# Scatter steps in one row and one branch for a pair's second block, in an expert stage on one core

## The chip, the cores and the metric

One of the eight cores of a Trainium2 chip runs the whole program. The metric is the device time of one execution in microseconds (us); a time without a name is a median over the runs.

## The reference, cut to what matters

Two layers of a diffusion backbone on 512 tokens of width 1024, in fp32. Layer 0 mixes tokens by a gated DeltaNet, layer 1 by a short gated convolution; after each mixer comes a mixture of SwiGLU experts, and a last RMSNorm ends the whole. The change lies in the experts alone. A router gives each token 2 of 32 experts, so 1024 rows of work in all. Expert e does, for its rows h (normed and modulated), with w1 and w3 of 1024 x 512 and w2 of 512 x 1024:

```
y = (silu(h @ w1[e]) * (h @ w3[e])) @ w2[e]
x[token] += weight * gate * y
```

## The kernel before, in words

`moe(l)` (L1454) runs once a layer: layer 0 from about 620 to 1130 us, layer 1 from about 1361 to 1865. The code is written out pair by pair for 16 pairs of experts. Pair p holds experts 2p and 2p + 1. Of each expert 64 rows stand in the pair's **first block** (128 rows); the two experts use two halves of 64 columns of TensorE at the same time, so each product is a row of matmuls that alternate between x = 0 and 1. If an expert of the pair has more than 64 rows (`n > 64`), a **second block** of 128 rows is computed too, under `tc.If`, a branch that every engine takes for itself. In this data that is so for 2 of the 30 pairs of the loop: pair 12 of layer 0 and pair 4 of layer 1. Pair 15 stands behind the loop and isn't changed.

A first block goes through these steps, with the lines at which the trace shows the work:
- **gate_up** (L1493, ends in ACT's Silu, L1499): 32 matmuls of h with w1 of both experts.
- **lin_up** (L1493, ends in DVE's product g = lin * silu, L1502): 32 matmuls with w3. `side` lets other steps run between them: the matmuls come in eight groups (k = 0 to 7), and a step stands behind each k that is named.
- **turn_g** (L1508, L1510): four transposes of g and a copy by ACT.
- **turn** (L1479, L1485 on DVE and its like on ACT): the next pair's gathered rows hg, transposed by eight matmuls and modulated into hT.
- **down** (L1520): 32 matmuls with w2; then DVE weighs the result, ACT and POOL split it into yhi and ylo (L1530, L1531).
- **scatter** of the pair's result, done within the next pair: eight steps, each of two matmuls with a selection matrix (L1556 yhi, L1557 ylo) into a PSUM bank and an add by DVE into the tokens xs (L1558).

All weights come in **units** of one 128 x 4096 tile: per pair two of w1, two of w3, two of w2, one for each expert. Nine buffers in three rings hold them. `issue(done)` (L162) goes through a fixed order of units and sends on SP's queue the load of every next unit (`load_unit`, L215) whose ring has a buffer that is free once the units before number `done` are used up. `next_unit(hold)` calls `issue(taken - hold)` and hands out the next unit. On the chip the load waits by semaphore until the engine that read the buffer is done; where the reader stands under a branch that isn't taken, PE raises the semaphore when it passes the branch.

The order of the instructions on each engine is the order of the code (a manual schedule). A pair of before:
1. next_unit twice (reissues the down buffers of pair p - 1), gate_up;
2. branch 1 (L1626): turn of hx to hTx, gate_up of the second block into gx;
3. next_unit twice (reissues the two gate buffers), lin_up with scatter steps of pair p - 1 behind groups 1, 3 and 5;
4. branch 2 (L1633): lin_up of the second block;
5. gather of hg for pair p + 2 on POOL, `issue(taken)` (reissues the two lin buffers), the five scatter steps left;
6. next_unit twice, out() (new yhi, ylo, sel);
7. branch 3 (L1642): turn_g, down and scatter of the second block;
8. turn_g, turn of the next rows, more(p + 2) (reads the count of pair p + 2 and gathers its second rows if there are any), down.

After the loop, a branch at L1665 covers the blocks beyond the second ones (`rest`), and isn't taken here.

Of the kernel before, what the change touches and what calls it, by code (L numbers as in the profile page):

```python
# [34 lines left out]
class Net:  # L35
# [83 lines left out]
    def plan(self):  # L119
# [18 lines left out]
        def moe(l):  # L138
            for p in range(16):
                for n in ("w1", "w3", "w2"):  # L140
                    order.extend((n, l, 2 * p + x) for x in range(2))
        moe(0)
        for g in range(2):
            order.extend(("w_in_b", 3072, u + g, 0) for u in (0, 2, 4))
            if g == 0:
                order.extend(("ada_w", 6144, 4 * b + u, l) for l, b in self.later for u in range(4))
        order.extend(("w_out_b", 1024, u, 0) for u in range(2))
        moe(1)

        self.place = {o: "B" for o in order if o[0] in ("ada_w", "w_in_b") or o[:2] == ("w2", 0) and o[2] > 29}  # L150
# [1303 lines left out]
    def moe(self, l):  # L1454
        tc, nc, I = self.tc, self.nc, self.I
        with ExitStack() as ms:
# [7 lines left out]
            def gather(gi, hg=None, skip=False, of=None):  # L1464

                if hg is None:
                    hg = wk.tile([128, 1024], F32, name="hg", bufs=2)
                of = self.hscr if of is None else of
                nc.gpsimd.indirect_dma_start(out=hg, out_offset=None, in_=of[:, :],
                                             in_offset=bass.IndirectOffsetOnAxis(ap=gi, axis=0),  # L1470
                                             **(dict(bounds_check=of.shape[0] - 1, oob_is_err=False) if skip else {}))
                return hg

            def turn(hg, to=None):

                hT = (wk.tile([128, 1024], F32, name="hT") if to is None else to).rearrange("p (k d) -> p k d", k=8)
                ps = [self.bank("tr") for _ in range(2)]
                for c in range(8):
                    nc.tensor.transpose(ps[c // 4][:, 128 * (c % 4):128 * (c % 4) + 128], hg[:, c::8], self.ident)  # L1479
                for c in range(8):  # L1480
                    q = ps[c // 4][:, 128 * (c % 4):128 * (c % 4) + 128]
                    if c > 3:
                        nc.scalar.activation(hT[:, c], q, AF.Identity, bias=self.m8[:, l, 2, c:c + 1], scale=self.m8[:, l, 0, c:c + 1])  # L1483
                    else:
                        nc.vector.tensor_scalar(hT[:, c], q, self.m8[:, l, 0, c:c + 1], self.m8[:, l, 2, c:c + 1], op0=OP.mult, op1=OP.add)  # L1485
                return hT

            def up(hT, w, side=()):

                ps = self.bank("pj")  # L1490
                for k in range(8):
                    for x in range(2):
                        nc.tensor.matmul(ps[64 * x:64 * x + 64], hT[:, k, 64 * x:64 * x + 64], w[x][:, k], start=(k == 0), stop=(k == 7))  # L1493
                    for _ in range(side[1].count(k) if side else 0):
                        next(side[0], None)
                return ps

            def gate_up(hT, w, g, side=()):
                nc.scalar.activation(g, up(hT, w, side), AF.Silu)  # L1499

            def lin_up(hT, w, g, side=()):
                nc.vector.tensor_tensor(g, up(hT, w, side), g, op=OP.mult)  # L1502

            def turn_g(g, gT=None):

                pg = self.bank("tr")
                for k in range(4):
                    nc.tensor.transpose(pg[:, 128 * k:128 * k + 128], g[:, k::4], self.ident)  # L1508
                gT = wk.tile([128, 4, 128], F32, name="gT") if gT is None else gT[:, :512].rearrange("p (k d) -> p k d", k=4)
                nc.scalar.activation(gT, pg.rearrange("p (k d) -> p k d", k=4), AF.Copy)  # L1510
                return gT

            def down(gT, w, ti, wi, o, y, eng=nc.gpsimd):

                self.sel(o, ti)
                for n in range(2):
                    py = self.bank("pj")
                    for k in range(4):
                        for x in range(2):
                            nc.tensor.matmul(py[64 * x:64 * x + 64], gT[:, k, 64 * x:64 * x + 64], w[x][:, k, 512 * n:512 * n + 512],  # L1520
                                             start=(k == 0), stop=(k == 3))
                    weigh(py, n, wi, y)
                    split(n, o, y, eng)
# [17 lines left out]
            def ident(x1):  # L1541
                for t in range(4):
                    nc.tensor.matmul(x1[t], self.ident, self.xs[:, t, 512:], start=True, stop=False)
                    yield

            def scatter(*a):
                for _ in scatter_parts(*a):
                    pass

            def scatter_parts(yhi, ylo, sel, ns=(0, 1)):  # L1550
                for n in ns:
                    for t in range(4):
                        ps = self.bank("pj")
                        c = slice(512 * n, 512 * n + 512)
                        s = sel[:, 128 * t:128 * t + 128]
                        nc.tensor.matmul(ps, s, yhi[:, c], start=True, stop=False)  # L1556
                        nc.tensor.matmul(ps, s, ylo[:, c], start=False, stop=True)  # L1557
                        nc.vector.tensor_tensor(self.xs[:, t, c], ps, self.xs[:, t, c], op=OP.add)  # L1558
                        yield n, t

            def col(t, c):
                return t[:, c:c + 1]

            gx = wk.tile([128, 512], F32, name="gx")

            def out():
                return tuple(wk.tile([128, m], F32R, name=n) for n, m in (("yhi", 1024), ("ylo", 1024), ("sel", 512)))

            def count(p):
                return nc.values_load(self.cnt[0:1, p], min_val=0, max_val=512)  # L1570
            hx = [wk.tile([128, 1024], F32, name=f"hx{i}") for i in range(2)]

            def more(p):
                n = count(slice(p, p + 1))
                with tc.If(n > 64):
                    gather(col(self.gxc, 16 + p), hx[p % 2])
                return n
# [33 lines left out]
            hgs = [gather(col(self.gxc, p)) for p in range(2)]  # L1611
# [3 lines left out]
            hT = turn(hgs.pop(0))  # L1615
# [4 lines left out]
            prev = None  # L1620
            for p in range(15):
                n = ns.pop(p)
                w = self.next_unit(), self.next_unit(1)
                g = wk.tile([128, 512], F32, name="g")
                gate_up(hT, w, g, () if p else (route, range(8)))
                with tc.If(n > 64):  # L1626

                    hTx = turn(hx[p % 2], hx[p % 2])
                    gate_up(hTx, w, gx)
                w = self.next_unit(), self.next_unit(1)  # L1630
                add = scatter_parts(*prev) if prev else iter(())
                lin_up(hT, w, g, (add, (1, 3, 5)))
                with tc.If(n > 64):  # L1633
                    lin_up(hTx, w, gx)
                if p < 14:
                    hgs.append(gather(col(self.gix, p + 2), skip=True))
                    self.issue(self.taken)
                for _ in add:
                    pass
                w = self.next_unit(), self.next_unit(1)  # L1640
                prev = out()
                with tc.If(n > 64):  # L1642
                    down(turn_g(gx, hx[p % 2]), w, col(self.tid, 16 + p), col(self.wsl, 16 + p), prev, gx)
                    scatter(*prev)
                gT = turn_g(g)
                hT = turn(hgs.pop(0))
                if p < 13:
                    ns[p + 2] = more(p + 2)
                prev = out()
                down(gT, w, col(self.tid, p), col(self.wsl, p), prev, g, nc.gpsimd if p < 14 else nc.vector)  # L1650

            n = count(slice(15, 16))
            w = self.next_unit(), self.next_unit(1)
            g = wk.tile([128, 512], F32, name="g")
            add = scatter_parts(*prev, ns=(1, 0))
            gate_up(hT, w, g, (add, (2, 3, 3, 4, 5, 6, 7)))
            w = self.next_unit(), self.next_unit(1)
            x1 = [self.bank("pj") for _ in range(4)]
            add = chain(add, ident(x1))
# [17 lines left out]
            prev = out()  # L1677
# [252 lines left out]
```

## Time and profile before

| what | before |
|---|---|
| median of 3 runs | 1875.29 us |
| the runs | 1871.93 to 1875.86 us |
| the profiled execution | 1876.28 us |
| its span in the trace | 1874.2 us |
| mean granted clock of TensorE in it | 0.964 of full speed |

The rest of the profile is a page and a trace of that one execution. Times in its rows count from the start of the span. The engines are PE (TensorE matmuls), PEld (its weight loads), DVE, ACT, POOL and SP; a q behind a name (PEq, SPq) is the engine's sequencer, which issues DMAs, branches and semaphore events. L1493 is line 1493 of the kernel.

### The profile page before, as it was taken

What the parts mean: (1) busy time and instruction counts of PE and PEld (TensorE: products, weight loads), DVE (VectorE), ACT (ScalarE), POOL (GpSimd) and SP (SyncE); (2) the same over time, 40 slices, a digit from 0 to 9 for tenths busy, and PEclk for the clock granted to TensorE, in tenths of its full rate; (3) what the DMA queues carried; (4) which work ended last, traced back from release to release, by engine and by line L of the source; (5) the groups of instructions that cost most, each with busy time, mean ns of one, the idle gap of its engine ahead of it and who ended that gap; (6) DMA issues with size and microseconds to landing.
All of it is one profiled execution on the core that took longest, in us unless ns stands there. A gap on an engine that the chain in (4) does not pass through costs nothing. (4 is left out here: it accounts for less than half of the span.)

```text
span 1874.2 us, 26554 instructions
## 1 busy us (share of the span) xinstructions
PE 1709.8 (91%) x10229; PEld 977.8 (52%) x10230; DVE 814.8 (43%) x1611; ACT 483.3 (26%) x888; POOL 415.4 (22%) x297
## 2 busy tenths in 40 slices
PE   5999988997988799999999988999799999999997
PEld 4766667776866344434434336688534344344332
DVE  5435877746664332323323237633523233233233
ACT  4465354523223111111111115223211111111112
POOL 1114464635410101111010103343111111110100
PEclk9999989998998899999999998999899999999998
DMA  9569975779835899999998953714589969999993
GB/s 330 192 241 339 293 222 157 173 170 262 244 107 227 345 425 425 427 425 426 426 425 346 404 193 139 279 40 180 226 340 427 425 268 425 426 425 425 426 418 123
DMA packets 154551, 572.33 MB, mean 305 GB/s; under 512 B 55208, under 2 KB 79961, under 8 KB 126214
## 3 DMA queue, kind: packets, MB, share of 16 engines
q1 hardware_dynamic: 148326, 555.26, 77.6%
q0 software_dynamic: 4896, 10.48, 1.5%
q10 hardware_dynamic: 1152, 4.19, 0.5%
q8 instruction: 115, 1.88, 0.4%
q14 instruction: 62, 0.51, 0.1%
HBM read 550.86 MB, written 26.38 MB: 308 GB/s over the span
## 5 line engine op out<-in xcount | busy, mean ns | idle before, releaser
L1493 PE MATMUL pj<-w,hT 128*64 128x512 f32 x2048 | 482.7, 602 | 7.1 <-DMA w<-in_w 2.5
L1558 DVE TENSOR_TENSOR xs<-pj,xs 128x512 f32<-128x512 f32 x264 | 170.5, 687 | 372.9 <-PE pj L1557 369.1
L1493 PEld LDWEIGHTS pj<-w,hT 128*64 128x64 f32 x2048 | 151.4, 137 | 266.1 <-issue 251.3
L1531 POOL TENSOR_TENSOR ylo<-g,yhi 128x512 fp32r<-128x512 f32 x56 | 70.8, 1265 | 653.4 <-ACT yhi L1530 653.4
L1520 PE MATMUL pj<-w,gT 128*64 128x512 f32 x960 | 212.6, 594 | 3.0 <-DVE hT L1485 1.6
L666 POOL TENSOR_TENSOR wlo<-w,whi 128x1024 fp32r<-128x1024 f32 x43 | 106.5, 2479 | 230.2 <-ACT whi L664 228.7
L1520 PEld LDWEIGHTS pj<-w,gT 128*64 128x64 f32 x960 | 78.1, 137 | 116.5 <-issue 108.8
L1526 DVE SCALAR_TENSOR_TENSOR g<-pj,wsl,gate 128x512 f32<-128x512 f32 x64 | 48.0, 751 | 177.7 <-PE pj L1520 164.1
L1556 PE MATMUL pj<-yhi,sel 128*128 128x512 f32 x264 | 117.5, 445 | 4.9 <-PEq L1633 4.2
L1510 ACT ACTIVATE gT<-tr 128x512 f32<-128x512 f32 x32 | 19.1, 598 | 383.5 <-PE tr L1508 383.5
L1556 PEld LDWEIGHTS pj<-yhi,sel 128*128 128x128 f32 x264 | 49.4, 187 | 120.0 <-issue 90.4
L681 PE MATMUL pj<-w,whi 128*128 128x512 f32 x336 | 105.7, 394 | 0.6 <-ACT whi L664 0.6
L1557 PE MATMUL pj<-ylo,sel 128*128 128x512 f32 x264 | 104.3, 395 | 1.3 <-POOL ylo L1531 1.3
L681 PE MATMUL pj<-hhi,wlo 128*128 128x512 f32 x224 | 93.7, 419 | 8.3 <-POOL wlo L666 7.0
L681 PE MATMUL pj<-hhi,whi 128*128 128x512 f32 x224 | 93.4, 417 | 6.4 <-DVE cv L797 5.5
L681 PE MATMUL pj<-hlo,whi 128*128 128x512 f32 x224 | 91.5, 409 | 0.0
L1530 ACT ACTIVATE yhi<-g 128x512 fp32r<-128x512 f32 x62 | 39.2, 632 | 193.3 <-DVE g L1526 193.3
L681 PEld LDWEIGHTS pj<-w,whi 128*128 128x128 f32 x336 | 63.7, 190 | 15.2 <-ACT whi L664 1.0
L664 ACT ACTIVATE whi<-w 128x1024 fp32r<-128x1024 f32 x53 | 55.3, 1054 | 53.9 <-PE pj L681 37.6
L1499 ACT ACTIVATE g<-pj 128x512 f32<-128x512 f32 x32 | 19.1, 598 | 190.5 <-PEq L1626 141.1
L681 PE MATMUL pj<-w,wlo 128*128 128x512 f32 x168 | 66.3, 394 | 0.0
L1483 ACT ACTIVATE hT<-tr,m 128x128 f32<-128x128 f32 x128 | 48.3, 458 | 55.2 <-PE tr L1479 53.5
(613 smaller groups left out, 2692.1 us busy)
## 6 DMA issues: line engine op xcount, KB each, us to landing
w<-in_w SPq DMA_DIRECT2D x188, 2048.0 KB
w<-in_ada_w SPq DMA_DIRECT2D x20, 2048.0 KB
w<-in_w_in_a SPq DMA_DIRECT2D x8, 2048.0 KB
w<-in_w_in_b SPq DMA_DIRECT2D x6, 2048.0 KB
w<-in_ada_w SPq DMA_DIRECT2D x8, 1024.0 KB
w<-in_w SPq DMA_DIRECT2D x8, 1024.0 KB
Y<-R SPq DMA_DIRECT2D x20, 256.0 KB
vp<-vscr SPq DMA_DIRECT2D x18, 256.0 KB
```

Of the source, the lines that this page charges most:

```text
L664: nc.scalar.activation(hi[:, :, :n], w, AF.Copy)
L666: (lo_eng or nc.gpsimd).tensor_tensor(lo[:, :, :n], w, hi[:, :, :n].bitcast(F32), op=OP.subtract)
L681: nc.tensor.matmul(out, n[j][0][:, k], n[j][1][:, k, a:b], start=(i == 0), stop=(i == 23))
L1483: nc.scalar.activation(hT[:, c], q, AF.Identity, bias=self.m8[:, l, 2, c:c + 1], scale=self.m8[:, l, 0, c:c + 1])
L1493: nc.tensor.matmul(ps[64 * x:64 * x + 64], hT[:, k, 64 * x:64 * x + 64], w[x][:, k], start=(k == 0), stop=(k == 7))
L1520: nc.tensor.matmul(py[64 * x:64 * x + 64], gT[:, k, 64 * x:64 * x + 64], w[x][:, k, 512 * n:512 * n + 512], start=(k == 0), stop=(k == 3))
L1526: nc.vector.scalar_tensor_tensor(y, py, wi, self.gate[:, 512 * n:512 * n + 512], op0=OP.mult, op1=OP.mult)
L1530: nc.scalar.activation(o[0][:, c], y, AF.Copy)
L1531: eng.tensor_tensor(o[1][:, c], y, o[0][:, c].bitcast(F32), op=OP.subtract)
L1556: nc.tensor.matmul(ps, s, yhi[:, c], start=True, stop=False)
L1557: nc.tensor.matmul(ps, s, ylo[:, c], start=False, stop=True)
L1558: nc.vector.tensor_tensor(self.xs[:, t, c], ps, self.xs[:, t, c], op=OP.add)
```

## The change

It touches the loop over pairs 0 to 14 alone. Behind gate_up, lin_up runs without side work; then come the gather for p + 2, all eight scatter steps of pair p - 1, and out(). One branch holds the whole second block: turn, gate_up, lin_up, turn_g, down and scatter. The four units of lin and down are taken with a hold of 2 to 5, so that none of these calls reissues a buffer of this pair, and `issue(self.taken - 4)` finds none either. `issue(self.taken - 2)` behind the branch reissues the four buffers of gate and lin.

```diff
                 gate_up(hT, w, g, () if p else (route, range(8)))
+                wl = self.next_unit(2), self.next_unit(3)
+                lin_up(hT, wl, g)
+                if p < 14:
+                    hgs.append(gather(col(self.gix, p + 2), skip=True))
+                    self.issue(self.taken - 4)
+                if prev:
+                    scatter(*prev)
+                wd = self.next_unit(4), self.next_unit(5)
+                prev = out()
                 with tc.If(n > 64):
 
                     hTx = turn(hx[p % 2], hx[p % 2])
                     gate_up(hTx, w, gx)
-                w = self.next_unit(), self.next_unit(1)
-                add = scatter_parts(*prev) if prev else iter(())
-                lin_up(hT, w, g, (add, (1, 3, 5)))
-                with tc.If(n > 64):
-                    lin_up(hTx, w, gx)
-                if p < 14:
-                    hgs.append(gather(col(self.gix, p + 2), skip=True))
-                    self.issue(self.taken)
-                for _ in add:
-                    pass
-                w = self.next_unit(), self.next_unit(1)
-                prev = out()
-                with tc.If(n > 64):
+                    lin_up(hTx, wl, gx)
+                    w = wd
                     down(turn_g(gx, hx[p % 2]), w, col(self.tid, 16 + p), col(self.wsl, 16 + p), prev, gx)
                     scatter(*prev)
+                w = wd
+                self.issue(self.taken - 2)
                 gT = turn_g(g)
```

## Rows read from the trace of the kernel before

**Rows 1.** The page: part 1 (engines), part 2 (40 slices), part 6 (DMA issues).

```profile
PE 1709.8 (91%) x10229; PEld 977.8 (52%) x10230; DVE 814.8 (43%) x1611; ACT 483.3 (26%) x888; POOL 415.4 (22%) x297
...
DMA  9569975779835899999998953714589969999993
...
w<-in_w SPq DMA_DIRECT2D x188, 2048.0 KB
```

**Rows 2.** Windows: from:to, us, busy PE, PEld, DVE, ACT, POOL; PEclk, DMA share, GB/s.

```profile
639.00:951.00 312.00, 300.13 (x1334) 127.02 (x1330) 95.07 (x168) 43.67 (x88) 39.82 (x34) 1.00 1.01 426
...
1373.60:1375.80 2.20, 2.10 (x10) 0.79 (x8) 0.07 (x1) 0.47 (x1) 0.00 (x0) 1.00 0.03 7
1531.00:1535.80 4.80, 4.80 (x26) 1.97 (x24) 0.75 (x1) 0.63 (x1) 1.27 (x1) 1.00 0.00 0
1535.80:1537.80 2.00, 2.00 (x12) 0.71 (x10) 0.75 (x1) 0.63 (x1) 0.36 (x1) 1.00 0.65 147
...
1539.80:1829.00 289.20, 281.60 (x1250) 115.93 (x1246) 94.49 (x165) 39.71 (x80) 30.87 (x27) 1.00 1.00 424
```

**Rows 3.** Timeline of PE, one pair: start, us, operation, count, idle before and its releaser.

```profile
652.46 9.15 PE L1493 MATMUL pj<-w,hT 128*64 128x512 f32 x40
661.54 0.50 PE L1556 MATMUL pj<-yhi,sel 128*128 128x512 f32 x1
...
662.20 1.94 PE L1493 MATMUL pj<-w,hT 128*64 128x512 f32 x8
...
669.36 0.47 PE L1556 MATMUL pj<-yhi,sel 128*128 128x512 f32 x1 [0.16 <-PEq L1633]
...
672.04 0.72 PE L1508 MATMUL tr<-ident,g 128*128 128x128 f32 x4
...
674.23 7.09 PE L1520 MATMUL pj<-w,gT 128*64 128x512 f32 x32
681.12 1.45 PE L1493 MATMUL pj<-w,hT 128*64 128x512 f32 x5
```

**Rows 4.** Timeline of PE: pair 11, taken pairs, last pairs, the branch L1665.

```profile
951.62 3.08 PE L1493 MATMUL pj<-w,hT 128*64 128x512 f32 x6 [2.46 <-DMA w<-in_w]
...
974.68 7.07 PE L1493 MATMUL pj<-w,hT 128*64 128x512 f32 x32
...
1010.26 7.09 PE L1520 MATMUL pj<-w,hx 128*64 128x512 f32 x32 [0.69 <-ACT hx L1510]
...
1118.20 2.83 PE L1538 MATMUL pj<-w,gT 128*64 128x512 f32 x6 [5.21 <-PEq L1665]
...
1479.27 7.07 PE L1493 MATMUL pj<-w,hT 128*64 128x512 f32 x32
...
1800.78 1.94 PE L1493 MATMUL pj<-w,hT 128*64 128x512 f32 x8 [0.16 <-PEq L1626]
```

**Rows 5.** Timeline of SP's queue: refills of weight buffers, two at a time.

```profile
635.12 0.82 SPq L215 DMA_DIRECT2D w<-in_w  x2
...
642.50 0.80 SPq L215 DMA_DIRECT2D w<-in_w  x2
...
659.65 0.81 SPq L215 DMA_DIRECT2D w<-in_w  x2
...
1375.82 0.81 SPq L215 DMA_DIRECT2D w<-in_w  x2
...
1383.20 0.81 SPq L215 DMA_DIRECT2D w<-in_w  x2
...
1535.82 0.81 SPq L215 DMA_DIRECT2D w<-in_w  x2
...
1542.82 0.80 SPq L215 DMA_DIRECT2D w<-in_w  x2
```

**Rows 6.** Timeline of DVE: the adds of the five scatter steps in a row.

```profile
670.16 3.08 DVE L1558 TENSOR_TENSOR xs<-pj,xs 128x512 f32<-128x512 f32 x5
```

**Rows 7.** One line, L1665: count, ns (least/median/most), first and last start.

```profile
L1665 PEldq COMPARE_BRANCH  x2: 3591/4913/6235, 1111.5 to 1845.5; - x2
```

## The prediction, made before the change was run

> **What bounds the kernel now.** I began with the page's shares and slices [rows 1]: PE works 91% of the span, and the DMA row holds two long stretches of nines, which are the expert stages of the two layers. The windows over them [rows 2] say more than the mean: from 639 to 951 us and from 1539.8 to 1829 the DMA engines are busy at a share of 1.00 or more, at 424 to 426 GB/s, without a break, while PE is busy 96 to 97% of the same time. Two limits run side by side there. A pair loads six units of 2.097 MB (2048 KB an issue [rows 1]) and a gather of about 0.5 MB: 13.1 MB, at 425 GB/s **30.8 us**. PE's pair, read from the timeline of a pair whose second block is skipped, lasts 681.12 - 652.46 = **28.66 us** [rows 3]. So PE eats up, pair after pair, the lead that the nine buffers gave it at the start of a layer. In layer 0 the lead is gone at 951.62: PE waits 2.46 us for the second lin unit of pair 11, and the six matmuls behind the wait take 3.08 us where 6 x 0.215 = 1.29 is usual [rows 4] (1.8 us more). In layer 1 the taken second block comes early (pair 4, from 1479.27), the queue drains meanwhile (0 GB/s from 1531 to 1535.8 [rows 2]) and starts afresh; no wait for weights shows, but the lead is nearly used up at the end. I check that by counting. From the first refill of layer 0, whose transfer starts some 2 us after its issue at 635.12 [rows 5], to the landing at 951.62 there are 61 units: 314.4 us, 5.15 us a unit. From 1537.8 (restart in layer 1) to the second lin unit of pair 14 there are 51 units: 262.7 us, so it lands at 1800.5; that product starts (its last part, after the branch) at 1800.78 [rows 4]. Slack there: 0.3 us by this count, and I allow 0 to 1.2.
>
> What follows from this: in layer 0 up to pair 11, and in layer 1 from pair 5 to pair 14, what the transfers do decides, and time saved on PE is worth nothing by itself. Only pairs after these points, and pairs 0 to 3 of layer 1, turn PE time into time.
>
> **The change, part by part.**
>
> PE, pair not taken (28 of 30). A product of 32 matmuls with nothing between takes 681.12 - 674.23 = 6.89 [rows 3]. Before, gate, the first branch and 8 lin matmuls take 661.54 - 652.46 = 9.08, against 40 x 0.215 = 8.61: 0.47 for the branch and the change of operands. Five steps in a row with the third branch take 672.04 - 669.36 = 2.68, at most 0.54 a step; one between the lin matmuls costs 662.20 - 661.54 = 0.66 and another change behind it. After: three products 20.67, five steps and one branch 2.68, three more steps at 0.54 1.61, and the unchanged stretch from turn_g to down 674.23 - 672.04 = 2.19: together 27.15. **Saving 1.5 us a pair.** Pair 0 of a layer has nothing to scatter and saves only the 0.47.
>
> DVE and PSUM. The adds of five steps take 3.08, 0.62 each [rows 6], PE's step 0.54 or less, so eight adds trail PE by some 1.5 us at the end of the row. The 2.19 of turn_g and turn cover that; the transposed g doesn't wait for them, the half of hT that DVE evacuates may, by 0 to 0.6. I take 0.2 and leave it inside the rounding. Without that cover the price is the 1.5.
>
> POOL: the gather for p+2 is issued one branch earlier, and costs nothing as before. SP: the instructions are the same, six issues a pair; what moves is when they can go. This is the main term.
>
> **The refills.** Before, the two buffers of gate were reissued when gate and its branch were over (659.65 in the pair of rows 3, 7.2 us into it), those of lin after the second branch. Now next_unit is called with a hold of 2 to 5, so it issues nothing, and all four go with issue(taken - 2) behind the single branch, 18 us into the pair. Where the DMA queue still holds other units, this costs nothing: five units of later work stand in it then. It costs where the queue is empty: at the first refill of a layer, and after the taken pair.
> - Layer 0: the first refill goes at about 642.2 (lin's end and the branch; its own refill went at 642.50) in place of 635.12 [rows 5]: **+7.0** on the whole unbroken chain of transfers. PE's pairs 1 to 10 save nothing, they wait more. Pair 11's lin starts at 951.62 + 7.0. The rest of that pair saves 1.15 (three interleaved steps and two branches): +5.85 at pair 12's gate. Its lin now follows gate at once, at 974.68 + 5.85 + 6.9 = 987.4, and its second unit lands 30.8 after the last one: 989.4 by the mean; 0 to 2, I take +1.0.
> - Pair 12, taken: it saves the interleaving, about 0.9. It pays where the scatter steps covered something: turn_g of gx follows lin_up of gx directly and waits for DVE's product; today five steps stand there and still 0.69 is left before the down product at 1010.26 [rows 4]. I take +1.0 (0.69 for the product, and the hand-over), and +0.7 for the turn of hx, whose DVE half now stands behind eight adds. Sum +0.8. Pairs 13 and 14: -1.5 each. Layer 0: 7.0 - 1.15 + 1.0 + 0.8 - 3.0 = **+4.65**, from 2.5 to 6.5.
> - Layer 1, start: the queue is really empty there (7 GB/s from 1373.6 to 1375.8 [rows 2]). First refill 1375.82, now 0.3 before the second of today (1383.20 [rows 5]): +7.1 on the chain. PE saves 0.5 + 3 x 1.5 = 5.0 until pair 4's gate, 1474.3; lin wants its second unit at 1481.2. Nineteen units of 5.15 from 1378 give 1475.9, with the delay 1483.0: a wait of 1.8, and up to 1.8 more as after 951.62; I take 2.5. Pair 4 itself +0.8, as above. So its end, and the refill of its down buffers (1535.82 before), comes at 1535.82 - 5.0 + 2.5 + 0.8 = 1534.1.
> - Layer 1, after the taken pair: its gate and lin refills can still go inside the block, as before, but all of them have landed when the block ends. The two down units are read by 1534.1 + 2 + 10.3 = 1546.4. Before, the next two came at 1542.82, in time. Now four come together at pair 5's branch: 1533.3 + 2 x 6.89 + 4.3 + 0.3 = 1551.7, and pick-up takes 2 (147 GB/s in the first two us of the restart before). The queue is empty for 7.3, and the chain stands at -1.7 + 7.3 = **+5.6**, from 4 to 7. Less the slack of 0.3 to 1.2: +4.9 to 5.3 at pair 14's lin, whose rest saves 1.0. Layer 1: **+4.2**, from 2 (less slack lost) to 8 (a slow stretch of 1.8 behind one or two waits).
>
> Sum: 4.65 + 4.2 = **+8.9 us**. The profiled execution took 1876.28 us, its span 1874.2 and 2.1 around it; the median of the runs is 1875.29, 1.0 lower. 1876.28 + 8.9 = 1885.2, by the median **1884.2**.
>
> **The price of the single branch.** No row shows a skip of this size: it passes over 124 matmuls with 124 weight loads, against 52 and 52 for the longest of today, inside the 2.68. The near row is that one, the far row the branch over the rest blocks, which took 3.6 and 6.2 us on PE [rows 7] and held PE 5.21 us up at 1118.20 [rows 4]. I take the near one, since the skipped code lies in line and is 2.4 times, not many times, as long. The other end is a rival.
>
> The Trainium skill, in Runtime: NRT & Kernel Launch, section Instruction fetch mechanics, says that code comes in blocks of 256 instructions, two of which are at hand, and that a taken branch to outside them waits for a fetch. By it a skip of 248 lands in the next block at most, and stalls only if that block isn't there yet: the sum stays 1884 if it is, and goes to the rival's if it isn't. No row here shows the blocks.
>
> **The rivals.**
> - Faster: *the late refill is hidden.* If the transfers still queued (or the lead) covered the delays, the savings would count where PE leads: -1.15 + 0.8 - 3.0 + (waits gone) in layer 0, about -3.3, and -1.8 in layer 1, whose chain still bounds pair 14: -5.1, **1870.2**. It decides if the queue has over 7 us of work at 635 and at 1376. Against it: 7 GB/s just before 1375.82. For it: before 635 the DMA row is still high. 0.10.
> - No change: *layer 1's transfers have room.* Per byte alone a unit takes 2.097/0.424 = 4.95, and 51 units then end 10 us before pair 14 wants them. If the rest of the 5.15 is gathers that move aside, layer 1's +4.2 turns into about -4 and the sum is +0.7: **1876**. Against it: the share of 1.00. 0.14.
> - Slower by far: *PE stalls at the single branch for code* in each of the 28 skips, by 2.6 to 5.2: +73 to +146, about **1950** or more; even half the skips would add 36. 0.08.
> - That the change doesn't do what it says has no room here: the order of PE's work is written out.
>
> **How the numbers follow.** My forecast has 0.68. Within 0.2% is within 3.75 us, about what a measurement of this kernel can tell from no change: 1871.5 to 1879.0. Faster is the first rival, 0.10; same is the second and the lowest end of the forecast, 0.14 + 0.02; slower is the rest of the forecast and the third, 0.66 + 0.08 = 0.74. The range: below, layer 0 at 2.5 with layer 1 at -2.3 (most of the second rival's gain missed) gives +0.2, so 1875.5; above, 6.5 + 8 = 14.5 with a part of it counted twice at pair 12, and a little for the branch, 1893. Outside lie the first and the third rival, 0.18.
>
> **What would show it.** Right: SP's refills come in fours, about 18 us into each pair; the gap of the DMA row after pair 0 is 7 us longer in both layers, and a new one of 7 us stands in pair 5 of layer 1; PE's pairs last 27.1 where it waits for nothing; PE has waits for w at the start of lin, from about pair 5 of layer 0 and from pair 9 of layer 1 on, with slow matmuls behind the longer ones. Wrong: no gap after pair 0, or gaps but no waits for w in layer 1 (second rival); PE idle at the merged branch by over 1 us (third); pairs not shorter than 28, which would undo the 1.5.

## The result, and the profile after

The median of four runs is **1887.26 us** (1883.36 to 1888.95), that of before 1874.51 in four runs (1871.93 to 1875.86): a ratio of 1.0067, 95% interval 1.005 to 1.0083, 12.75 us slower. The forecast was 8.9 us slower, a median of 1884.2 in a range of 1875.5 to 1893. The profiled execution of after is the fastest of its four, 1883.36 us with a span of 1881.6, 7.4 over the span of before. One execution of a later kernel, early_8, ran at a granted clock of 0.557 and is left out of its numbers.

The page of after, parts 1 and 2 (the slices that answer to [rows 1]):

```profile
PE 1682.4 (89%) x10229; PEld 972.5 (52%) x10230; DVE 808.7 (43%) x1611; ACT 482.1 (26%) x888; POOL 415.6 (22%) x297
...
DMA  9579975679926799999998774714579988999994
```

PE does the same 10,229 matmuls in 27 us less, and the kernel is slower. In the DMA row the slices in which the two expert stages begin (the 14th and the 30th) fall from 8 to 7. The windows of after (columns as in [rows 2]):

```profile
636.50:642.30 5.80, 5.69 (x28) 1.67 (x24) 0.00 (x0) 0.00 (x0) 0.00 (x0) 1.00 0.01 4
648.00:959.00 311.00, 284.94 (x1296) 119.11 (x1292) 88.82 (x162) 41.41 (x83) 39.80 (x34) 0.99 1.01 426
1380.00:1387.80 7.80, 7.70 (x36) 2.51 (x34) 0.29 (x1) 0.60 (x1) 0.00 (x0) 1.00 0.01 2
...
1565.00:1829.00 264.00, 246.26 (x1124) 103.16 (x1122) 79.26 (x145) 35.86 (x73) 30.75 (x26) 0.99 1.01 426
...
835.50:839.50 4.00, 4.00 (x10) 1.24 (x12) 0.00 (x0) 0.00 (x0) 0.00 (x0) 0.50 1.01 429
...
1555.00:1560.20 5.20, 3.90 (x19) 2.89 (x17) 4.84 (x9) 0.60 (x1) 0.00 (x0) 1.00 0.28 54
```

4 GB/s for 5.8 us in pair 0 of layer 0, 2 GB/s for 7.8 in pair 0 of layer 1, 54 GB/s for 5.2 in pair 5 of layer 1: the three gaps that were forecast. Behind each the DMA is as full as before. SP's timeline (as [rows 5]) says why:

```profile
642.32 0.83 SPq L215 DMA_DIRECT2D w<-in_w  x2
...
670.20 1.75 SPq L215 DMA_DIRECT2D w<-in_w  x4
...
1387.83 0.81 SPq L215 DMA_DIRECT2D w<-in_w  x2
```

642.32 answers to 635.12 before, 1387.83 to 1375.82 (in a layer that starts 5.4 later); the two lines show the first two refills of each pair 0, and the other two follow at once. In the next pair four refills go together at 670.20, 17.9 us behind the start of the pair's gate (652.28). The waits of PE by line (sum, times, longest), and PE's timeline of that pair and in pairs 7 and 11 of layer 0:

```profile
PE tr L1479 <- DVEq L1635: 30.1, 26, 1.2
PE pj L1493 <- DMA w<-in_w: 20.3, 13, 4.0
```

```profile
652.28 13.93 PE L1493 MATMUL pj<-w,hT 128*64 128x512 f32 x64
...
670.23 0.72 PE L1508 MATMUL tr<-ident,g 128*128 128x128 f32 x4
672.10 1.13 PE L1479 MATMUL tr<-ident,hg 128*128 128x128 f32 x8 [1.15 <-DVEq L1635]
...
680.08 2.31 PE L1493 MATMUL pj<-w,hT 128*64 128x512 f32 x10
...
835.49 9.64 PE L1493 MATMUL pj<-w,hT 128*64 128x512 f32 x30 [3.83 <-DMA w<-in_w]
...
959.16 8.78 PE L1493 MATMUL pj<-w,hT 128*64 128x512 f32 x30 [3.99 <-DMA w<-in_w]
```

From gate to gate this pair takes 680.08 - 652.28 = 27.80 us, the next ones 27.78. Weights are waited for 13 times in place of once. Pair 11's second lin unit is taken at 959.16; before it was 951.62 [rows 4], so the 7.2 of the first refill are still there 61 units later, as 7.5. Behind the wait that ends at 835.49, 30 matmuls take 9.64 us where 30 x 0.215 = 6.45 is usual: the granted clock of 835.5 to 839.5 is 0.50, the lower level of 1.2 GHz, after 3.8 us in which PE stood; the same costs 2.3 us behind the wait of pair 11. The other line is a second new wait, 1.15 us in each of 26 pairs: the turn of the next rows waits until **DVE** has passed the single branch (L1635). DVE's timeline has the eight adds ahead of that, 666.93 to 671.8 (as [rows 6]):

```profile
666.93 4.86 DVE L1558 TENSOR_TENSOR xs<-pj,xs 128x512 f32<-128x512 f32 x8
```

The branch itself is cheap on PE, 0.34 us at the median and 0.38 at most (ns, as [rows 7]):

```profile
L1635 PEldq COMPARE_BRANCH  x32: 70/337/375, 637.8 to 1819.3; - x32
```

### The profile page after: what moved, and what is told of

Same layout as the page of the kernel before. It is cut to its first block, busy times and chain, and to the rows that moved or that the text cites. A ratio compares the mean times of both kernels' runs of the same rounds, so it can differ in the third digit from the quotient of the medians.

```text
span 1881.6 us, 26073 instructions
## 1 busy us (share of the span) xinstructions
PE 1682.4 (89%) x10229; PEld 972.5 (52%) x10230; DVE 808.7 (43%) x1611; ACT 482.1 (26%) x888; POOL 415.6 (22%) x297
## 5 line engine op out<-in xcount | busy, mean ns | idle before, releaser
L1493 PE MATMUL pj<-w,hT 128*64 128x512 f32 x2048 | 473.4, 603 | 20.4 <-DMA w<-in_w 20.3
L1502 DVE TENSOR_TENSOR g<-pj,g 128x512 f32<-128x512 f32 x32 | 22.1, 691 | 431.2 <-PE pj L1493 417.6
L1558 DVE TENSOR_TENSOR xs<-pj,xs 128x512 f32<-128x512 f32 x264 | 162.3, 679 | 15.0 <-PE pj L1557 15.0
L1520 PEld LDWEIGHTS pj<-w,gT 128*64 128x64 f32 x960 | 68.0, 137 | 122.3 <-issue 118.3
L1556 PE MATMUL pj<-yhi,sel 128*128 128x512 f32 x264 | 108.8, 412 | 0.7 <-DVE g L1526 0.4
L1479 PE MATMUL tr<-ident,hg 128*128 128x128 f32 x256 | 38.7, 294 | 42.3 <-DVEq L1635 30.1
```

## The experiments

Executions of one kernel differ by up to 9 us, and in the traces a layer starts at another time in each; so the table has two columns from the traces beside the medians: from the first gate matmul of pair 0 to that of pair 15, for each layer. All ratios are to the kernel before, run on the same chip (medians 1873.8 to 1874.5).

| kernel | median us | ratio, 95% interval | layer 0 | layer 1 |
|---|---|---|---|---|
| before | 1873.8 | | 465.5 | 458.8 |
| after | 1887.26 | 1.0067 (1.005 to 1.0083) | 472.3 | 462.4 |
| row_only | 1863.62 | 0.9948 (0.993 to 0.9967) | 460.0 | 453.0 |
| merge_only | 1890.05 | 1.0087 (1.0068 to 1.0105) | 474.3 | 466.5 |
| after_act | 1885.59 | 1.0068 (1.0047 to 1.009) | 471.5 | 463.8 |
| after_p0_p5 | 1880.35 | 1.0039 (1.0025 to 1.0053) | 472.1 | 459.0 |
| late_p0 | 1879.67 | 1.0033 (1.0022 to 1.0044) | 471.8 | 458.5 |
| early_8 | 1887.0 | 1.0058 (1.0042 to 1.0075) | 467.1 | 467.0 |
| two_branch_row | 1865.29 | 0.9954 (0.9939 to 0.9969) | 463.5 | 452.1 |
| after_scatter_first | 1886.80 | 1.0068 (1.0043 to 1.0094) | 469.6 | 459.1 |
| two_branch_first | 1869.06 | 0.9968 (0.9954 to 0.9981) | 462.6 | 453.7 |
| before_scatter_first | 1864.74 | 0.9939 (0.9917 to 0.9962) | 461.7 | 453.0 |
| split_5_3 | 1861.48 | 0.9934 (0.992 to 0.9948) | 460.2 | 451.2 |

The layers of early_8 are from its repeat, below.

### The two parts of the change, each by itself

**row_only**, before with the row:

```diff
-                add = scatter_parts(*prev) if prev else iter(())
-                lin_up(hT, w, g, (add, (1, 3, 5)))
+                lin_up(hT, w, g)
...
-                for _ in add:
-                    pass
+                if prev:
+                    scatter(*prev)
```

> The kernel before with one part of the change: all eight scatter steps in one row behind the second branch, three branches and the early refills kept. Theory (the loss comes from the late refills, the row itself saves): PE's pair about 27.7 us in place of 28.66, no wait of PE for DVE at turn, since that wait belongs to the single branch; the transfers keep their times in layer 0 (wait at 951.6 as before), the gain counts behind it and in layer 1: 6 to 10 us under before, about 1866. Rival (eight adds in a row hold PE up wherever they stand): pair 28.5 or more, time within 2 us of before.

10.2 us faster, just over the 6 to 10 that were expected. A pair without a wait for weights lasts 27.58, and PE goes from turn_g to turn with no wait for DVE, although the same eight adds stand behind lin. PE's timeline, same places as above:

```profile
698.21 0.72 PE L1508 MATMUL tr<-ident,g 128*128 128x128 f32 x4
698.77 0.62 PE L1479 MATMUL tr<-ident,hg 128*128 128x128 f32 x4
```

So the row is a gain, and the wait for DVE belongs to the single branch.

**merge_only**, after with the scatter steps as they were:

```diff
-                lin_up(hT, wl, g)
+                add = scatter_parts(*prev) if prev else iter(())
+                lin_up(hT, wl, g, (add, (1, 3, 5)))
...
-                if prev:
-                    scatter(*prev)
+                for _ in add:
+                    pass
```

> The changed kernel with the scatter steps put back as they were (three between the lin matmuls, five behind), so only the single branch and with it the late refills are new. Theory: the first refill of each layer 7 us later, waits for lin weights as in the changed kernel, 10 to 16 us over before (1885 to 1891), not better than the changed kernel. Rival (the row of scatter steps is what costs, by DVE's adds): within 2 us of before.

16.3 us slower, as the theory has it, and slower than after. The single branch is the loss: 16 us with the steps between, 24 with the row (1863.6 to 1887.3). Alone it gives PE next to nothing: a pair takes 28.43 us against 28.67, since turn_g now waits 0.30 for an add and turn 0.59 for DVE's branch:

```profile
670.62 0.72 PE L1508 MATMUL tr<-ident,g 128*128 128x128 f32 x4 [0.30 <-DVE xs L1558]
671.94 1.13 PE L1479 MATMUL tr<-ident,hg 128*128 128x128 f32 x8 [0.59 <-DVEq L1636]
```

### Is it the wait for DVE or the refills?

**after_act**: in the branch's turn, ACT evacuates all eight pieces, so DVE has nothing in those PSUM banks.

```diff
-                    hTx = turn(hx[p % 2], hx[p % 2])
+                    hTx = turn(hx[p % 2], hx[p % 2], -1)
```

(turn takes the last piece of DVE as a third argument, 3 as before.)

> The changed kernel, but the turn inside the branch is evacuated by ACT alone, so that PE's next turn no longer waits until DVE has passed the branch behind its eight adds. Theory (late refills): the waits of 1.15 us a pair go, pairs without a wait for weights last 26.7 in place of 27.8, but the time follows the transfers and falls by 0 to 4 us under the changed kernel (1883 to 1887). Rival (these 26 waits, 30.1 us in sum, are the loss): at least 13 us under the changed kernel, 1874 or less.

The 26 waits are gone and the pairs take 27.0, but the time stays where it was (1885.6, and 0.8 less and 1.4 more in the two layers). Most of what was a wait for DVE became a wait for weights, as the waits of PE show (20.3 + 30.1 before this edit):

```profile
PE pj L1493 <- DMA w<-in_w: 36.9, 16, 3.7
```

Behind the longer waits the matmuls also ran slower: on the page PE is busy for 1691.2 us, against 1682.4 in after, with the same matmuls. So taking away 30 us of PE's waits for DVE was worth less than 2 us: the transfers set the time.

**late_p0**, the opposite test: before, with the new form in pair 0 of each layer only.

```diff
+                if p == 0:
...
+                else:
...
```

(The new form stands under the `if`, the form of before under the `else`.)

> The kernel before with the new form in pair 0 of each layer alone; pair 0 has nothing to scatter, so its single branch and the refill behind it are all that is new, in 2 of 30 pairs. Theory (where the queue is empty, one late refill shifts all later transfers): layer 0's first refill 7 us late and, 61 units on, its wait in pair 11 too; pairs 0 to 15 of layer 0 take 6 to 8 us more; layer 1 nothing, since pair 4's lin comes 16 us after its gate there and the queue starts afresh behind it. 6 to 8 us over before, 1880 to 1882. Rival (the loss comes by small pieces from every pair: DVE's adds at the branch, code, clock): at most 1 us over before.

5.9 us slower, from two pairs of thirty, and all of it in layer 0 (+6.3; layer 1 -0.3), just under the 6 to 8 that were expected. The windows and PE's timeline repeat what after shows, with the old code from pair 1 on:

```profile
635.50:641.40 5.90, 5.76 (x28) 1.72 (x24) 0.02 (x1) 0.00 (x0) 0.00 (x0) 1.00 0.01 3
647.00:957.00 310.00, 296.37 (x1296) 125.58 (x1292) 92.56 (x162) 41.49 (x83) 39.84 (x34) 1.00 1.01 426
```

```profile
957.67 1.93 PE L1493 MATMUL pj<-w,hT 128*64 128x512 f32 x6 [1.64 <-DMA w<-in_w]
```

From the issue of the first refill to the landing of the unit that pair 11's lin waits for (61 units, by the semaphore events of the traces), the times are 316.5 us in before, 316.8 in after, 316.8 in merge_only, 317.1 in after_act, 316.2 here. It is nearly one number, whatever PE does in between: that shows that a late chain didn't catch up. The Trainium skill, in DMA: Bandwidth & Descriptors, section Where 436 GB/s comes from, gives 435 GB/s as the ceiling of the 16 ports into the on-chip memory, and says that the HBM side, about 358, binds in transfers from HBM. The 424 to 426 of these windows are 2% under the first figure and well over the second, and the measurement decides.

### Where must the refills be early?

**after_p0_p5**: after, with the form of before in pairs 0 and 5, where after has its gaps.

```diff
+                if p in (0, 5):
...
+                else:
...
```

> The changed kernel with the form of before (three branches, refills early) in pairs 0 and 5 of each layer alone, the two places where the DMA queue is empty. Theory: the first refill goes at 635 again, no gap in pair 5 of layer 1, no chain delayed: the whole loss goes and the savings of PE stay where they count: 2 to 6 us under before (1869 to 1873). Rival (the loss is spread over all pairs, by the late refills everywhere, the branch or DVE's adds): of some 12 us, 11 stay, 1884 to 1887.

Only half the loss went, and what is left stands in layer 0 (+6.6; layer 1 +0.2); both theories fell. The first refill is early again, but the gap has moved on to pair 1, whose four refills wait for its branch at 669.9 (the line shows three of them). SP's timeline and the windows:

```profile
669.89 1.28 SPq L215 DMA_DIRECT2D w<-in_w  x3
```

```profile
668.50:673.00 4.50, 3.22 (x20) 2.43 (x20) 3.46 (x7) 0.66 (x2) 0.00 (x0) 1.00 0.54 137
...
1413.50:1418.50 5.00, 3.70 (x23) 2.79 (x23) 3.96 (x8) 0.60 (x1) 0.00 (x0) 1.00 0.45 102
```

The last queued unit lands at 668.5, before the refill at 669.9. So near the start of a layer, where PE leads by all nine buffers, what is queued there is less than the 18 us by which the refills come late; the runs show the queue empty in pair 0 (after) and in pair 1 (here).

**early_8**: the same with the form of before in pairs 0 to 3 and 5 to 8.

```diff
-                if p in (0, 5):
+                if p < 4 or 4 < p < 9:
```

> The changed kernel with the form of before in pairs 0 to 3 and 5 to 8 of each layer, the new form in the others. Theory, amended after the run with pairs 0 and 5: a refill 18 us into a pair leaves the queue empty in every pair in which PE's lead is still near its full size, not in the first alone, so early refills in one pair only move the gap to the next; the backlog grows by 2 to 3 us a pair, and by the landings of before the last queued unit ends 2 us before pair 1's late refill, but 2 after pair 2's, 5 after pair 3's, and in layer 1 5 after pair 9's. So four pairs behind each start are enough: no chain late by more than 1 us, 2 to 6 us under before (1868 to 1872). Rival (late refills cost in all pairs, or the new form itself does): 1880 or more, as with pairs 0 and 5.

The time is no better, 1880.9 to 1889.4 where 1868 to 1872 was expected. A second run was to show whether transfers or PE are late.

> The same kernel once more, for a trace at the usual clock: its runs before took 1881 to 1889 where the amended theory gave 1868 to 1872. If the theory of the empty queue is right, a stretch without transfers must still stand somewhere behind a late refill (in pairs 0 to 5 of a layer, or where the form changes), or unit 70's landing in layer 0 must come more than 317 us after the first refill. If the queue is never empty and the landings keep their times, the loss lies in PE: waits at the branch or for code where the two forms alternate, seen as idle PE outside the waits for weights.

1885.08 us in this one run. In layer 0 the queue does its work: 315.4 us from first refill to the 61st landing. The list of PE's waits names no weights in either layer. In layer 1, which starts 2 us late, the units up to pair 14's land at most 5 us later than before, but for the four that pair 4, the taken one, sends for, and PE doesn't wait for those either. So that part of the amended theory holds, if not to the 1 us that was expected: the transfers no longer hold PE up. PE is late by itself, in the new-form pairs behind pair 8. PE's timeline in pairs 9 and 10:

```profile
902.42 0.69 PE L1479 MATMUL tr<-ident,hg 128*128 128x128 f32 x4 [1.16 <-DVEq L1656]
904.52 0.60 PE L1479 MATMUL tr<-ident,hg 128*128 128x128 f32 x4 [1.41 <-issue]
...
934.50 0.58 PE L1479 MATMUL tr<-ident,hg 128*128 128x128 f32 x2 [1.35 <-issue]
935.51 9.62 PE L1520 MATMUL pj<-w,gT 128*64 128x512 f32 x32 [0.43 <-issue]
```

PE stops in the middle of eight transposes that wait for nothing, and behind the second stop the down product runs at a slow clock (9.62 us where 7.09 is usual; granted clock 0.73 from 935.5 to 945). In the window 902 to 903.5 the DMA view has one packet on the instruction queue among the weights:

```profile
q1 hardware_dynamic: 39, 0.56, 89.1%
q8 instruction: 1, 0.02, 4.6%
```

There are four such stops, two in each layer, 5.2 us in sum; the layers are 9.8 us longer than before's, and the slow products behind three of the stops and the waits for DVE at turn are in that too. This looks like code that isn't there yet behind the branch, but that isn't shown. Such a packet stands behind the branch in after, at 908 us, with no stop, so its presence alone doesn't prove it; which pairs stop and why only in this kernel stays open. The Trainium skill, in Runtime: NRT & Kernel Launch, section Instruction fetch mechanics, says that a taken branch out of the two blocks at hand waits for a fetch. The four stops of 1.1 to 1.4 us would fit it; after had no such stop in 28 skips of the same 248 instructions, and no run here shows the blocks.

**two_branch_row** settles what early_8 could not: after with branch 1 kept in every pair, so that gate's buffers alone are early.

```diff
+                with tc.If(n > 64):
+
+                    hTx = turn(hx[p % 2], hx[p % 2])
+                    gate_up(hTx, w, gx)
-                wl = self.next_unit(2), self.next_unit(3)
+                wl = self.next_unit(), self.next_unit(1)
                 lin_up(hT, wl, g)
...
                 with tc.If(n > 64):
-
-                    hTx = turn(hx[p % 2], hx[p % 2])
-                    gate_up(hTx, w, gx)
                     lin_up(hTx, wl, gx)
```

> The changed kernel with branch 1 kept (turn and gate_up of the second block behind gate_up), so that the two gate buffers are reissued as early as before; the row of eight steps behind lin and the single branch for the rest, which still holds the lin buffers, stay. Theory (gate's refill alone keeps the queue filled, lin's may come late): first refill at 635, 316 us from there to the wait in pair 11, 4 to 10 us under before, 1864 to 1870. Rival (lin's late refill, or the branch behind the row, costs as much): 1878 or more.

1865.29: this one branch takes 22 us off the changed kernel. The first refills go early again (SP's timeline), lin's in pair 0 at 641.83, and the 61 units take 317.3. The wait for DVE is gone too, since the turn whose banks DVE empties stands at the early branch (pairs of 27.39).

```profile
634.44 0.83 SPq L215 DMA_DIRECT2D w<-in_w  x2
...
641.83 0.80 SPq L215 DMA_DIRECT2D w<-in_w  x2
```

### Where the row stands

**after_scatter_first**: after, with the row ahead of lin_up.

```diff
+                if prev:
+                    scatter(*prev)
                 lin_up(hT, wl, g)
...
-                if prev:
-                    scatter(*prev)
```

> The changed kernel with the row of eight scatter steps put ahead of lin_up instead of behind it; branch and refills stay late. Theory: the first refill of a layer goes some 7 us late as in the changed kernel and lin waits for the same landings, but 4 us of scatter now lie before that wait and not behind it, and DVE's adds run under lin, so turn waits for no branch: pairs of 26.7 where nothing is late, 5 us less behind the last wait of each layer, 11 to 20 us under the changed kernel, 1867 to 1876. Rival (place of the row is without weight, only the number of branches and the late refills count): within 3 us of the changed kernel, 1884 or more.

1886.8, as after: the expectation fell. In the trace both layers are shorter than after's, by 2.7 and 3.3, not 5 and more, and what they gained was lost behind pair 15, where this profile takes 56.7 us (granted clock 0.88) and after's 50.5 (0.93). The wait for DVE didn't go either. It moved one step, from turn to turn_g, which follows lin directly and now waits until DVE has multiplied g and passed the branch. Nearly all of it is the product: in the taken pairs of after, turn_g of gx waits 0.89 us for the same product, with no branch between. The sum of these waits in after_scatter_first:

```profile
PE tr L1508 <- DVEq L1635: 26.7, 28, 1.0
```

**two_branch_first** (two_branch_row with the row ahead of lin) and **before_scatter_first** (before with the row ahead of lin, three branches):

> Two branches: turn and gate_up of the second block behind gate_up as before, so that the gate buffers are reissued early; then the eight scatter steps in a row, lin_up, and one branch with the rest of the second block. Theory: the queue never runs empty in pair 0 or 1, the row lies ahead of the wait for lin weights and its adds under lin: at or below the run with the row behind lin (1863.6), 1856 to 1864. Rival (lin buffers reissued 18 us into the pair are late enough to empty the queue): a gap in pair 0 to 2 of a layer, 1870 or more.

> The kernel before with one edit: the eight scatter steps in a row between branch 1 and lin_up; three branches and early refills kept. Theory: as the run with two branches, but one more branch a pair (0.3 us where PE leads) and lin buffers reissued at about the same time: 1857 to 1865, 2 us or less from the run with two branches. Rival (the row ahead of lin delays the lin buffers' reissue by 4 us a pair and that empties the queue): 1868 or more.

1869.06 and 1864.74, slower than expected for the first; both pay 0.9 us a pair at turn_g (24.4 and 24.5 us in 28 waits), so the row ahead of lin is no better than behind it (1863.62 and 1865.29).

**split_5_3** takes both: five steps ahead of lin, three behind branch 2, three branches.

```diff
                 add = scatter_parts(*prev) if prev else iter(())
-                lin_up(hT, w, g, (add, (1, 3, 5)))
+                for _ in range(5):
+                    next(add, None)
+                lin_up(hT, w, g)
```

> A version that might beat both: three branches and early refills as before, five scatter steps in a row ahead of lin and three in a row behind branch 2. The three behind cover DVE's product, for which turn_g waited 0.9 us a pair where all eight stood ahead; the five ahead lie before the wait for lin weights. Theory: pairs of 27.3 where nothing is late, no wait of PE on DVE's branch, 1858 to 1864. Rival (place is without weight as long as refills are early): 1863 to 1866, as the runs with the row behind and ahead of lin.

1861.48 in five runs, 0.9934 of before: the fastest of all. PE's turn_g waits for its own branch only, 0.15, and the three steps behind lin cover DVE:

```profile
695.40 0.47 PE L1556 MATMUL pj<-yhi,sel 128*128 128x512 f32 x1 [0.16 <-PEq L1635]
...
697.17 0.72 PE L1508 MATMUL tr<-ident,g 128*128 128x128 f32 x4 [0.15 <-PEq L1644]
697.73 0.62 PE L1479 MATMUL tr<-ident,hg 128*128 128x128 f32 x4
```

Its lead over row_only (2.1 us) is less than the two intervals tell apart.

## Why the prediction was right

Direction, mechanism and range held, and the size was 3 to 4 us short by the medians: 12.75 against the forecast's 8.9, or 9.7 from the 1874.51 of four runs to 1884.2. Step by step:

- **The late first refill.** Forecast 642.2, measured 642.32; +7.0 on the chain, measured 7.5 at pair 11's lin. late_p0 shows it alone. The rival in which it is hidden fell with the 4 GB/s window; so did the one with room in layer 1, whose pairs 10 to 14 all wait for lin weights.
- **PE's saving a pair** was the step that failed: forecast 1.5, measured 28.67 - 27.78 = 0.9. Its sum of 27.15 for PE's own work was right: with the wait for DVE gone, after_act's pairs take 27.0. The text put the trailing adds under the 2.19 us of turn_g and turn, took 0.2, and gave 1.5 as the price without that cover. The turn doesn't need the adds' results, but its PSUM banks are also written in the branch's turn and emptied there by DVE, and DVE releases them only when it passes the branch, behind the eight adds: 1.15 us. Before, branch 1 let them go long before (row_only and two_branch_row, with as many adds in a row, have no such wait).
- **Layer 0.** Sum forecast +4.65, up to 6.5; measured 472.3 - 465.5 = 6.8. Pairs 13 and 14 saved 0.75 each in place of 1.5 (1.5 of the difference), and pair 11 gave no 1.15 back: its lin runs at a slow clock behind the 3.99 us wait, so pair 12's gate comes 7.1 late, not 5.85. Pair 12 was the other way, +0.6 for the forecast 1.8: its lin followed at once, with none of the 1.0 of waiting. The 0.6 left of the difference is that this layer starts 0.6 earlier than before's.
- **Layer 1.** Forecast +4.2, measured 3.6. Savings to pair 4's gate 3.5 (forecast 5.0, the same 0.9); wait for its lin 1.25 (1.8, taken as 2.5 with the clock); the transfers behind pair 5's branch 5.3 late against the layer's start (5.6), and 5.0 late at pair 14's second lin unit. That unit had 1.1 of slack before (0.3 to 1.2), and the rest of pair 14 saved 0.4 (1.0). The 5.6 was in part luck: the refill behind pair 4 came 1.0 later than forecast, by the smaller savings, and the empty stretch was 1.3 shorter. The working has two slips: by its own terms pair 5's gate starts at 1533.9 (1535.63 in the trace of before, less 1.7) and not at 1533.3, and 5.6 less 0.3 to 1.2 is 4.4 to 5.3.
- **The single branch on PE**: at most 0.38 us, near the near row; the rival with a stall at each skip fell for this kernel. Its sign, PE idle at the branch by over 1 us, did show, as the 1.15 at turn, but the cause was DVE (after_act). Whether the stops of early_8 are of that rival's kind isn't shown.
- **What the text had too narrow**: it named two places where a late refill costs, the start of a layer and the pair behind the taken one. Those are the places of the gaps in after, but with early refills there the next pair has the gap (after_p0_p5). Elsewhere, it says, five units of later work stand in the queue; near the start of a layer that isn't so.

The layers sum to 10.3 us in the profiled execution; it gained 1.6 behind pair 15, 0.8 between the layers and 0.6 ahead of layer 0, hence 7.4 in its span. Why the other three runs are 3 to 6 us slower than the profiled one isn't known, as they have no trace.

## What to carry to other kernels

Where a kernel runs at the DMA limit, ask of each edit when every prefetch buffer comes free, and set that time beside the landing of the last transfer queued: one refill that comes late to an empty queue moves all that follow, and PE time saved ahead of the next wait for weights doesn't count. Here a branch that wasn't taken still held what its body touches, weight buffers until PE had passed it and PSUM banks until DVE had; so keep apart bodies that release early what the next loads need.

## What the runs showed of the hardware

- A branch that DVE passes over with work queued ahead of it made PE wait at the turn behind it, though the turn needs nothing that was computed there: 0.59 us a pair in merge_only, 1.15 in after, none in after_act, where the branch's turn leaves DVE out.
- PE stopped four times for 1.1 to 1.4 us in early_8 at transposes that waited for nothing, with a 16 KB packet of code on the way; no other kernel's trace here has such a stop in the expert stages. The cause isn't shown.
- The slower clock is dear behind short waits: in after, 3.8 and 4.0 us of waiting for weights cost 3.2 and 2.3 us more in the matmuls behind them.
